# Two more 8 KB slots in a hybrid attention and expert layer: 27 in place of 25, from a smaller descriptor reserve and shared small tiles

## The chip, the cores and the metric

The kernel runs on one core of a Trainium2 chip. The metric is device time in microseconds, the median of several executions; lower is better.

## The reference, cut to what matters

One layer over 256 tokens of width 1024, in float32. Everything but the last step feeds the expert mixture, which reads 96 MB of weights (16 experts of three 2 MB matrices):

```python
xn = rms_norm(h, norm_mix_g)
sb_q, sb_k, sb_v, r_q, r_k, r_v, r_g = split(xn @ w_in)          # 1024 x 4608
y_sb  = stick_breaking_attention(sb_q, sb_k, sb_v) @ w_sb_out
y_ret = silu(r_g) * norm(retention_chunkwise(rotary(r_q), rotary(r_k), r_v)) @ w_ret_out
g_sb, g_ret = split(sigmoid(xn @ w_gate + b_gate))
h = h + (g_sb * y_sb + g_ret * y_ret) @ w_out
hn = rms_norm(h, norm_ffn_g)
# group: top 1 of 4; expert: top 2 of the 4 in the group; combine[t, e] is 0 for the others
for e in range(16):
    hidden = silu(hn @ w_exp_gate[e]) * (hn @ w_exp_up[e])       # 1024 x 512 each
    y = y + combine[:, e:e + 1] * (hidden @ w_exp_down[e])       # 512 x 1024
return rms_norm(h + y, norm_final_g)
```

## The kernel before, in words

SBUF is one pool of equal **slots** of 2048 float32 per partition (8 KB; 1 MB over 128 partitions), handed out by `take` (L120) and returned by `give` (L127). The list of free slots is a queue: the slot that was given back first is taken first. A load of weights, an intermediate result, a work space each take a slot. Small tiles (tables, counts, the router's intermediates) come from a second pool by `small` (L131); two small tiles with the same tag share a place.

Weights are read in tiles of one slot each. `plan` (L154) lists all loads in the order of use; `pump` (L157) issues the next ones, from SyncE's queue, as long as a slot is free and the number of loads so far is below a limit. The table `LIMIT` sets that limit by the number of dense units done (`set_limit`, L734), so that slots are left over for intermediates; from the output projection on (L769) there is no limit, and the free list alone decides. A load that was given the slot of a tile still being read waits on SyncE's queue for the last reader of that tile, and all later loads wait behind it. `drop` (L172) gives a weight tile back after its last use.

The **dense stage** (the first 240 us) splits each weight tile into two float32r halves (ACT copies, DVE subtracts: `split_parts`, L246) and multiplies with both (`mm_unit`, L270), the attention and retention steps between. Then the router ranks each token among its expert's tokens (`choose`, L844; `shares`, L1053). The **expert stage** (`head`, L1094, `tail`, L1145) goes over eight pairs of experts. For pair i the kernel computes the gate product (`proj`, L987: four tiles r = 0 to 3), the up product (four tiles) and, one pair later, the down product (four tiles, `down`, L1019); 64 tokens of each of the two experts form a block of 128 rows. This document calls the tiles of up of pair 0 "up tile 0 to 3 of pair 0", and so on. The order in which the tiles are loaded is gate 0, up 0, then gate i+1, down i, up i+1.

`places` (L951) builds the table that says which token stands in which of the 64 rows; `tables` (L958) transposes it on PE and copies the transpose, 256 columns, to a tile `S` (L972). `scatter` (L1043) multiplies by `S` to add the pair's outputs, `y2`, to the tokens' accumulators. There are two tiles S, used in turns. `after` (L974) runs when PE's products with a tile have been written down: it drops the tile, takes two slots out of those that come free in up of pair 0, one for work space and one for the products `y2`, and calls `pump`:

```python
if not work and key == ("u", 0, 0):
    w = take([P, 2048])
    work.update(b=..., ht=..., pb=..., S=[small([P, T], F32R, "S")])
if not y2 and key == ("u", 0, 3):
    w = take([P, 2048], F32R)
    y2.append(w[:, 0:1024].rearrange("p (h n) -> p h n", h=2))
    work["S"].append(w[:, 1024:1024 + T])
pump()
```

So S of even pairs is a small tile (1 KB, its place shared with `cmp` of `choose`), and S of odd pairs lies in the products' slot.

Of the kernel before, what the change touches and what calls it, by code (L numbers as in the profile page):

```python
# [9 lines left out]
F32 = mybir.dt.float32  # L10
F32R = mybir.dt.float32r
BF16 = mybir.dt.bfloat16
# [5 lines left out]
P = 128  # L18
T = 256
D = 1024  # L20
KC = D // P
NB = T // P
# [1 line left out]
CAP = 64  # L24
PLACE = 1024
EPS = 1e-6
SLOTS = 25

LIMIT = [
    (0, 17), (1, 20), (7, 21), (17, 22), (19, 23), (21, 24), (25, 25), (27, 26), (29, 27), (30, 30),  # L30
    (39, 31), (43, 32), (45, 38), (47, 39), (49, 40), (51, 41), (52, 44), (53, 45), (55, 46), (56, 47),
    (59, 48), (61, 49), (63, 50),
]


# [63 lines left out]
def layer(ctx: ExitStack, tc, cst, dec, prm, x, w_in, w_gate, w_sb_out, w_ret_out,  # L99
          w_out, w_exp_gate, w_exp_up, w_exp_down, out):  # L100
    nc = tc.nc
    pe, act, dve, pool, sp = nc.tensor, nc.scalar, nc.vector, nc.gpsimd, nc.sync
# [12 lines left out]

    free = list(range(SLOTS))
    held = {}
    uid = [0]

    def take(shape=(P, 2048), dt=F32):  # L120
        s = free.pop(0)
        uid[0] += 1
        t = big.tile(list(shape), dt, name=f"b{uid[0]}", tag=f"s{s}")
        held[id(t)] = (s, t)
        return t
# [5 lines left out]
    def small(shape, dt=F32, name=None, bufs=1, tag=None):  # L131
        uid[0] += 1
        return sm.tile(list(shape), dt, name=f"{name}_{uid[0]}", tag=tag or name, bufs=bufs)
# [23 lines left out]
    def pump():  # L157
        while loads and loaded[0] < limit[0] and free:
            key, shape, parts, hook = loads.pop(0)
            t = raws[key] = take(shape)  # L160
            loaded[0] += 1
            for i, (at, src) in enumerate(parts):
                sp.dma_start(t[at], src)
                if hook:
                    hook(i)
# [6 lines left out]
    def drop(key):  # L172
        give(raws.pop(key))
# [315 lines left out]
    key, shape, parts, hook = loads[2]  # L489
# [253 lines left out]
    i = 0  # L743
# [73 lines left out]
    L = small([P, NB, 20], F32, "L")  # L817
    L5 = L.rearrange("p b (g e) -> p b g e", g=5)
    E5 = [P, 5, 4, 4]
    cmp = small([P, NB, 80], F32, "cmp", tag="S")  # L820
    n5 = small([P, NB, 5, 4], F32, "n5")
    gl, en = L[:, :, 0:4], n5[:, :, 1:5, :]
    mask = small([P, NB, 4, 4], BF16, "mask")
# [20 lines left out]
    def choose(tb):  # L844
        stt(L[:, tb, :], lp[:, tb, 0:20], rh[:, tb:tb + 1], par[:, R_BR:R_BR + 20], op0=ALU.mult, op1=ALU.add)
        yield
        c = cmp[:, tb, :]
        c5 = c.rearrange("p (g i j) -> p g i j", g=5, i=4)
        tt(c5, L5[:, tb][:, :, None, :].to_broadcast(E5), L5[:, tb][:, :, :, None].to_broadcast(E5), op=ALU.subtract)
        yield  # L850
        c = c.rearrange("p (a b) -> p a b", b=16)
        tt(c, c, lt[:, None, :].to_broadcast([P, 5, 16]), op=ALU.is_ge)
        dve.tensor_reduce(n5[:, tb].rearrange("p g i -> p (g i)"), cmp[:, tb, :].rearrange("p (a j) -> p a j", j=4),
                          axis=AX.X, op=ALU.add)
        stt(mask[:, tb], en[:, tb], 2.0, n5[:, tb, 0, :][:, :, None].to_broadcast([P, 4, 4]), op0=ALU.is_lt,
            op1=ALU.is_gt)
        m2 = mk[:, tb].rearrange("p (i j) -> p i j", j=2)
        tt(either[:, tb], m2[:, :, 0], m2[:, :, 1], op=ALU.max)
        yield
# [25 lines left out]
    def rows_onto(q, tb):  # L885
        for h in range(2):
            pe.matmul(F[q][tb], identr, hn[h][:, tb, 512 * q:512 * q + 512], start=h == 0, stop=False,
                      skip_group_check=True)

    best, norm = choose(0), row_norm(1)  # L890
    next(best)
    next(norm)
# [10 lines left out]
    rows_onto(1, 0)  # L903
    act.activation(rank[:, 0, :], rp[0][:, 0:8], AF.Copy)
    list(choose(1))
    pe.matmul(rp[1][:, 0:8], tri, either[:, 1, :], start=False, stop=True)
    pe.matmul(rp[1][:, 8:16], ones, either[:, 0, :], start=True, stop=False)
# [13 lines left out]
    def selb(tb):  # L921
        return sel[:, tb, :, None].to_broadcast([P, 4, 4])
# [10 lines left out]
    y2, work, gs = [], {}, {}  # L933
# [40 lines left out]
    def after(key):  # L974
        drop(key)
        if not work and key == ("u", 0, 0):
            w = take([P, 2048])
            work.update(b=w[:, 0:512], ht=[w[:, 512 + 512 * k:1024 + 512 * k].rearrange("p (f s) -> p f s", f=4)
                                           for k in range(2)],
                        pb=w[:, 1536:1664].bitcast(BF16), S=[small([P, T], F32R, "S")])  # L980
        if not y2 and key == ("u", 0, 3):
            w = take([P, 2048], F32R)
            y2.append(w[:, 0:1024].rearrange("p (h n) -> p h n", h=2))
            work["S"].append(w[:, 1024:1024 + T])
        pump()

    def proj(i, which, ps, hook):  # L987
        o = 64 * (i % 4)
        for r in range(4):
            if hook:  # L990
                hook(r)
            w = raws[(which, i, r)]
            for k in range(2):
                c = 2 * r + k
                for j in range(2):
                    pe.matmul(ps[64 * j:64 * j + 64, :], xgt[:, c, o:o + 64], w[:, j, k, :],  # L996
                              start=c == 0, stop=c == KC - 1)
            after((which, i, r))
# [20 lines left out]
    def down(i, hook=None):  # L1019

        ht = work["ht"][i % 2]
        ys = [(bank(b), cs) for b, cs in zip("gm", pieces(i))]
        for r in range(4):
            if hook:
                hook(r)
            w = raws[("d", i, r)]
            j = r // 2
            for y, cs in ys:
                for k in range(2):
                    f = 2 * (r % 2) + k  # L1030
                    for q in range(2):
                        pe.matmul(y[64 * q:64 * q + 64, cs], ht[:, f, 64 * j:64 * j + 64],  # L1032
                                  w[:, k, 512 * q + cs.start:512 * q + cs.stop],
                                  start=r == 0 and k == 0, stop=r == 3 and k == 1)
            after(("d", i, r))
        for y, cs in ys:
            hilo(y2[0][:, 0, cs], y2[0][:, 1, cs], y[:, cs])
# [13 lines left out]
                                  start=False, stop=last and h == 1 and cs.stop == 512, skip_group_check=True)  # L1051

    def shares():  # L1053
        one = [small([P, NB, 4, 4], F32, f"one{k}") for k in range(2)]
        for k in range(2):
            for tb in range(NB):
                stt(one[k][:, tb], en[:, tb], float(k), selb(tb), op0=ALU.is_equal, op1=ALU.mult)
        v = small([P, 2, NB], F32, "v")
        pr = small([P, NB, 16], F32, "pr")
        of = [o.rearrange("p b g e -> p b (g e)") for o in one]  # L1060
        for k in range(2):
            tt(pr, L[:, :, 4:20], of[k], op=ALU.mult)
            dve.tensor_reduce(v[:, k, :], pr, axis=AX.X, op=ALU.add)
        gm = small([P, NB, 1], F32, "gm")
        dve.tensor_reduce(gm, gl, axis=AX.X, op=ALU.max)
        gd = small([P, NB, 4], F32, "gd")
        tt(gd, gl, gm.to_broadcast([P, NB, 4]), op=ALU.subtract)
        act.activation(gd, gd, AF.Exp)
        e2 = small([P, NB], F32, "e2")
        tt(e2, v[:, 1, :], v[:, 0, :], op=ALU.subtract)  # L1070
        act.activation(e2, e2, AF.Exp)
        yield
        gs = small([P, NB], F32, "gs")
        dve.tensor_reduce(gs, gd, axis=AX.X, op=ALU.add)
        den = small([P, NB], F32, "den")
        stt(den, e2, 1.0, gs, op0=ALU.add, op1=ALU.mult)
        dve.reciprocal(den, den)
        yield
        for tb in range(NB):
            c = cm[:, tb, :, 1:3]  # L1080
            pairs = "p (i j) -> p i j"
            stt(pr[:, tb, :], of[1][:, tb, :], e2[:, tb:tb + 1], of[0][:, tb, :], op0=ALU.mult, op1=ALU.add)
            dve.tensor_scalar(c, pr[:, tb, :].rearrange(pairs, j=2), den[:, tb:tb + 1], None, op0=ALU.mult)
            dve.tensor_copy(cm[:, tb, :, 0:1], rh[:, tb:tb + 1][:, :, None].to_broadcast([P, NE // 2, 1]))
        yield
        for a in range(3):
            part = cmb[:, :, :, a, :].rearrange("p b i c -> p (b i) c")
            rest = cm.rearrange("p b i c -> p (b i) c")
            dve.tensor_copy(part, rest)
            if a < 2:  # L1090
                tt(rest, rest, part, op=ALU.subtract)
        yield

    def head(first):  # L1094

        pt = pt0 if first else [onehot(0, tb, rank[:, tb, :]) for tb in range(NB)]
        parts = shares() if first else iter(())
        gather(0, pt, [0])

# [141 lines left out]
```

## Time and profile before

| | |
|---|---|
| median of 3 executions | 463.96 us (463.85 to 464.1) |
| the profiled execution, its own time | 464.75 us |
| its span, first to last instruction | 463.0 us |
| PE (matmul) busy | 443.4 us, 96% |
| PEld (weight loads) busy | 298.8 us, 65% |
| DVE, ACT, POOL busy | 186.9, 166.7, 22.2 us |
| bytes moved | 142.49 MB, mean 308 GB/s |

The profile is one execution. Engines are PE (matmul), PEld (its weight loads), DVE, ACT, POOL and SP (SyncE, whose queue issues the loads). A line such as L996 is a line of the kernel. The page's slices divide the span in 40 equal parts of 11.6 us. Matmuls are pipelined, their ends are modelled, and a float32 product stands as two records: a run of products is read by its first start and last end.

### The profile page before, as it was taken

Reading aid. Unit: us, or ns where it says so; the run is one execution under the profiler, and the core shown is the slowest. Engines: PE = TensorE matmul, PEld = TensorE weight load, DVE = VectorE, ACT = ScalarE, POOL = GpSimd, SP = SyncE. Lnnn points to the kernel's source line nnn. Section 1 sums busy time; section 2 is a strip of 40 time slices with the busy share of each in tenths; the row PEclk is TensorE's granted clock in tenths of the full one; section 3 lists DMA queues with packets and bytes.
Section 4 is the critical chain, followed back from the end, with each engine's and each line's share of the span. In section 5 each row is a group of like instructions: output and inputs, shape, how many; then the busy total and the mean of one; then the engine's idle time right before and its main releaser. Section 6 shows DMA issues by size and latency. Waiting matters only on the chain.

```text
span 463.0 us, 6743 instructions
## 1 busy us (share of the span) xinstructions
PE 443.4 (96%) x2715; PEld 298.8 (65%) x2715; DVE 186.9 (40%) x349; ACT 166.7 (36%) x246; POOL 22.2 (5%) x36
## 2 busy tenths in 40 slices
PE   7999999999999999999999999999989999999881
PEld 6699878888899999999996333333353333333240
DVE  4756487654457865578538410101031001010003
ACT  3643688895653655444543020101000010102003
POOL 2400110110002200000001000000000000000000
PEclk9999999999999999999999999999999999999997
DMA  8999975249302279995949999999999999999972
GB/s 282 353 382 392 388 250 172 90 121 316 107 1 92 92 237 372 408 398 183 368 159 335 346 370 390 410 408 411 408 409 410 409 410 409 409 408 409 410 288 97
DMA packets 58037, 142.49 MB, mean 308 GB/s; under 512 B 3344, under 2 KB 23952, under 8 KB 57872
## 3 DMA queue, kind: packets, MB, share of 16 engines
q1 hardware_dynamic: 57568, 141.35, 81.2%
q10 hardware_dynamic: 432, 0.65, 0.5%
q8 instruction: 23, 0.38, 0.3%
q14 instruction: 14, 0.11, 0.1%
HBM read 140.93 MB, written 1.05 MB: 307 GB/s over the span
## 4 chain that ended last, share of the span: by engine, by line
PE 80%; DMA 14%; DVE 2%; ACT 1%; issue 1%; POOL 1%; SPq 0%; ACTq 0%; DVEq 0%
PE p L294 20%; PE p L996 17%; PE p L1032 8%; PE p L281 8%; PE p L284 7%; PE p L282 7%; DMA b<-in_w_exp_down 6%; DMA b<-in_w_exp_up 5%; DMA b<-in_w_exp_gate 2%; PE p L945 2%; PE z L586 1%; PE p L1050 1%; DMA b<-in_x 1%; PE p L688 1%; PE p L629 1%
## 5 line engine op out<-in xcount | busy, mean ns | idle before, releaser
L253 DVE TENSOR_TENSOR b<-b,b 128x1024 fp32r<-128x1024 f32 x72 | 88.7, 1241 | 71.7 <-ACT b L251 70.6
L996 PE MATMUL p<-b,b 128*64 128x512 f32 x512 | 117.1, 597 | 0.2 <-DMA b<-in_w_exp_up 0.2
L294 PE MATMUL p<-b,b 128*128 128x512 f32 (+1 forms) x504 | 102.7, 359 | 0.5 <-ACT b L251 0.3
L251 ACT ACTIVATE b<-b 128x1024 fp32r<-128x1024 f32 x72 | 75.5, 1056 | 76.6 <-PE p L282 47.7
L294 PEld LDWEIGHTS p<-b,b 128*128 128x128 f32 x504 | 82.6, 190 | 14.6 <-ACT b L251 0.7
L996 PEld LDWEIGHTS p<-b,b 128*64 128x64 f32 x512 | 35.8, 137 | 68.1 <-issue 64.4
L281 PE MATMUL p<-b,b 128*128 128x256 f32 x288 | 71.6, 286 | 0.0
L282 PE MATMUL p<-b,b 128*128 128x256 f32 x288 | 70.7, 283 | 0.0
L1032 PE MATMUL p<-b,b 128*64 128x512 f32 (+1 forms) x288 | 57.8, 548 | 2.7 <-DMA b<-in_w_exp_down 1.9
L281 PEld LDWEIGHTS p<-b,b 128*128 128x128 f32 x288 | 55.1, 191 | 0.5
L282 PEld LDWEIGHTS p<-b,b 128*128 128x128 f32 x288 | 55.2, 192 | 0.0
L1032 PEld LDWEIGHTS p<-b,b 128*64 128x64 f32 x288 | 20.2, 137 | 38.5 <-issue 32.3
L284 PE MATMUL p<-b,b 128*128 128x256 f32 x288 | 41.1, 283 | 0.0
L573 DVE SCALAR_TENSOR_TENSOR b<-p,b 128x512 fp32r<-128x512 f32 (+1 forms) x13 | 7.4, 566 | 83.3 <-ACT b L572 83.3
L284 PEld LDWEIGHTS p<-b,b 128*128 128x128 f32 x288 | 37.4, 192 | 0.0
L1011 DVE SCALAR_TENSOR_TENSOR b<-p,share,b 128x512 f32<-128x512 f32 x8 | 6.0, 751 | 62.6 <-PE p L996 62.6
L572 ACT ACTIVATE b<-p 128x512 fp32r<-128x512 f32 (+1 forms) x13 | 6.4, 495 | 53.5 <-PE p L1032 52.9
L972 ACT ACTIVATE b<-p 128x256 fp32r<-128x256 bf16 x4 | 1.5, 386 | 38.1 <-PE p L971 38.1
L972 ACT ACTIVATE S<-p 128x256 fp32r<-128x256 bf16 x4 | 1.5, 384 | 37.4 <-PE p L971 37.4
L1006 ACT ACTIVATE b<-p,share 128x512 f32<-128x512 f32 x8 | 5.5, 688 | 21.3 <-PE p L996 21.3
L1017 ACT ACTIVATE b<-p 128x512 f32<-128x512 f32 x8 | 4.8, 597 | 22.9 <-PE p L1016 22.9
L1188 POOL TENSOR_TENSOR rf<-rf,mhalf 128x1 f32<-128x1 f32 x2 | 1.1, 542 | 208.1 <-DVE rf L1187 208.1
(172 smaller groups left out, 338.2 us busy)
## 6 DMA issues: line engine op xcount, KB each, us to landing
b<-in_w_exp_gate SPq DMA_DIRECT2D x64, 512.0 KB, 10.2
b<-in_w_exp_up SPq DMA_DIRECT2D x64, 512.0 KB, 10.2
b<-in_w_exp_down SPq DMA_DIRECT2D x31, 1024.0 KB, 12.7
b<-in_w_in SPq DMA_DIRECT2D x17, 1024.0 KB, 14.3
b<-in_w_gate SPq DMA_DIRECT2D x8, 1024.0 KB, 5.3
b<-in_w_ret_out SPq DMA_DIRECT2D x4, 1024.0 KB, 5.0
b<-in_w_out SPq DMA_DIRECT2D x4, 1024.0 KB, 11.5
b<-in_w_sb_out SPq DMA_DIRECT2D x2, 1024.0 KB, 9.4
```

Source lines behind the costliest of these rows:

```text
L251: act.activation(hi, raw, AF.Copy)
L253: tt(lo, raw, hi.bitcast(F32), op=ALU.subtract)
L281: pe.matmul(ps, wh[:, k, cs], h[:, k, :], start=k == 0, stop=False)
L282: pe.matmul(ps, wh[:, k, cs], l[:, k, :], start=False, stop=False)
L284: pe.matmul(ps, wl[:, k, cs], h[:, k, :], start=False, stop=k == nk - 1)
L294: pe.matmul(ps[tb], kth(a, k)[:, tb * P:(tb + 1) * P], b[:, j, :], start=n == 0 and k == 0, stop=n == 2 and k == KC - 1)
L572: act.activation(hi, src, AF.Copy)
L573: stt(lo, src, 1.0, hi.bitcast(F32), op0=ALU.mult, op1=ALU.subtract)
L945: pe.matmul(ps[:, c, :], hn[h][:, tb, features(c2, c)], pt[tb].rearrange("p e s -> p (e s)"), start=c == 0 and tb == 0 and h == 0, stop=c ...
L996: pe.matmul(ps[64 * j:64 * j + 64, :], xgt[:, c, o:o + 64], w[:, j, k, :], start=c == 0, stop=c == KC - 1)
L1011: stt(work["b"], u, gs[i][:, 0:1], work["b"], op0=ALU.mult, op1=ALU.mult)
L1032: pe.matmul(y[64 * q:64 * q + 64, cs], ht[:, f, 64 * j:64 * j + 64], w[:, k, 512 * q + cs.start:512 * q + cs.stop], start=r == 0 and k == ...
```

## The change

It makes 27 slots of 8 KB in place of 25. The room comes from two sides. The program is built with a reserve of 1 KB per partition for the descriptors of transfers that GpSimd would issue, in place of the default 16 KB. And small tiles are put together: both tiles S lie in the products' slot, which is now taken when up tile 1 of pair 0 is dropped, and no longer tile 3; `cmp` is one tile of 96 numbers for both blocks of tokens, in which the tiles `one` and `pr` of `shares` lie too. All limits rise by 2.

```diff
-SLOTS = 25
+SLOTS = 27
 LIMIT = [
-    (0, 17), (1, 20), (7, 21), (17, 22), (19, 23), (21, 24), (25, 25), (27, 26), (29, 27), (30, 30),
+    (0, 19), (1, 22), (7, 23), (17, 24), (19, 25), (21, 26), (25, 27), (27, 28), (29, 29), (30, 32),
...
-    cmp = small([P, NB, 80], F32, "cmp", tag="S")
+    cmp = small([P, 96], F32, "cmp")
...
-        c = cmp[:, tb, :]
+        c = cmp[:, 0:80]
...
-                        pb=w[:, 1536:1664].bitcast(BF16), S=[small([P, T], F32R, "S")])
-        if not y2 and key == ("u", 0, 3):
+                        pb=w[:, 1536:1664].bitcast(BF16))
+        if not y2 and key == ("u", 0, 1):
             w = take([P, 2048], F32R)
             y2.append(w[:, 0:1024].rearrange("p (h n) -> p h n", h=2))
-            work["S"].append(w[:, 1024:1024 + T])
+            work["S"] = [w[:, 1024 + T * k:1024 + T * k + T] for k in range(2)]
...
-        one = [small([P, NB, 4, 4], F32, f"one{k}") for k in range(2)]
+        one = [cmp[:, 32 * k:32 * k + 32].rearrange("p (b g e) -> p b g e", b=NB, g=4) for k in range(2)]
...
-        pr = small([P, NB, 16], F32, "pr")
+        pr = cmp[:, 64:96].rearrange("p (b e) -> p b e", b=NB)
...
-    nc = _bacc.Bacc("TRN2", target_bir_lowering=False, num_devices=1)
+    nc = _bacc.Bacc("TRN2", target_bir_lowering=False, num_devices=1, dynamic_dma_scratch_size=1024)
```

The order of instructions on each engine stays; what moves is the moment at which a load is written into the program, and with it the slot that it gets. On SyncE's queue, the loads of down of pair 1 (four) and of up of pair 2 (four, each in two halves) stood like this before. The first number in a tile's name counts tiles in the order in which the kernel's code makes them: a tile that is made earlier is one for which a slot came free earlier.

```order
L163 DMA b270_2569<-in_w_exp_down 128x2x1024
L163 DMA b271_2580<-in_w_exp_down 128x2x1024
L163 DMA b275_2597<-in_w_exp_down 128x2x1024
L163 DMA b279_2615<-in_w_exp_down 128x2x1024
L163 DMA b282_2630<-in_w_exp_up 128x1024 x2
L163 DMA b283_2637<-in_w_exp_up 128x1024 x2
L163 DMA b288_2661<-in_w_exp_up 128x1024 x2
L163 DMA b289_2668<-in_w_exp_up 128x1024 x2
```

And with the change:

```order
L163 DMA b263_2527<-in_w_exp_down 128x2x1024
L163 DMA b267_2548<-in_w_exp_down 128x2x1024
L163 DMA b269_2570<-in_w_exp_down 128x2x1024
L163 DMA b270_2581<-in_w_exp_down 128x2x1024
L163 DMA b277_2614<-in_w_exp_up 128x1024 x2
L163 DMA b278_2621<-in_w_exp_up 128x1024 x2
L163 DMA b280_2632<-in_w_exp_up 128x1024 x2
L163 DMA b281_2639<-in_w_exp_up 128x1024 x2
```

Before, the four down loads took the slots of gate tiles 2 and 3 and up tiles 1 and 2 of pair 0, and the work space and the products took those of up tiles 0 and 3 (names 273 and 280). With the change the four down loads take the slots of gate tiles 0 to 3 of pair 0, the work space and the products those of up tiles 0 and 1 (272 and 273), and the first load of up of pair 2 that of up tile 2; from the third on, each load has the slot that a load two places ahead of it had before.

On ACT the copies of the transposed place tables (L972) stood like this, with what each waits for in brackets (DMAHW: a transfer's landing); `b_2589` is the work space and `b_2621` the products' slot:

```order
L972 ACTIVATE S_2590<-p_2606 128x256 [waits PE_49]
L1006 ACT_TABLE_LOAD [waits DMAHW5_49,DMAHW4_49]
L1006 ACTIVATE b_2589<-p_2489,share_2602 128x512 [waits DVE_49]
L972 ACTIVATE b_2621<-p_2647 128x256 [waits DMAHW3_49,DMAHW2_49,PE_49]
L1017 ACTIVATE b_2589<-p_2651 128x512 [waits PE_49]
```

And with the change, where `b_2597` is the products' slot:

```order
L972 ACTIVATE b_2597<-p_2605 128x256 [waits DMAHW7_49,DMAHW6_49,PE_49]
L1006 ACT_TABLE_LOAD [waits DMAHW5_49,DMAHW4_49]
L1006 ACTIVATE b_2590<-p_2495,share_2601 128x512 [waits DVE_49]
L972 ACTIVATE b_2597<-p_2649 128x256 [waits PE_49]
L1017 ACTIVATE b_2590<-p_2653 128x512 [waits PE_49]
```

The first copy now goes to a slot that held a weight tile, so it waits for that tile's two transfers, which the second copy did before; no other wait is added.

## Rows read from the trace of the kernel before

**Rows 1.** The page's slices: PE's busy tenths, and GB/s moved.

```profile
PE   7999999999999999999999999999989999999881
...
GB/s 282 353 382 392 388 250 172 90 121 316 107 1 92 92 237 372 408 398 183 368 159 335 346 370 390 410 408 411 408 409 410 409 410 409 409 408 409 410 288 97
```

**Rows 2.** Waits of PE, 20 to 245 us: total, times, longest.

```profile
PE p L553 <- POOL rxp L317: 0.5, 1, 0.5
```

**Rows 3.** PE's timeline, 418 to 453 us: start, us, instruction, records, [idle before].

```profile
418.03 6.71 PE L996 MATMUL p<-b,b 128*64 128x512 f32 x26
424.96 1.93 PE L996 MATMUL p<-b,b 128*64 128x512 f32 x6 [0.22 <-DMA b<-in_w_exp_up]
...
427.84 4.17 PE L996 MATMUL p<-b,b 128*64 128x512 f32 x16
432.74 1.94 PE L1032 MATMUL p<-b,b 128*64 128x512 f32 x8 [0.72 <-DMA b<-in_w_exp_down]
...
437.07 0.66 PE L1016 MATMUL p<-identr,b 128*128 128x128 f32 x4
...
440.32 1.94 PE L1032 MATMUL p<-b,b 128*64 128x512 f32 x8 [0.63 <-DMA b<-in_w_exp_down]
442.98 1.95 PE L1032 MATMUL p<-b,b 128*64 128x256 f32 x16 [0.71 <-ACT b L572]
...
445.98 5.94 PE L1032 MATMUL p<-b,b 128*64 128x256 f32 x48
```

**Rows 4.** The chain that ended last, its end: start, us, what.

```profile
421.14 11.46 DMA b<-in_w_exp_down
...
434.68 15.69 DMA b<-in_w_exp_down
...
450.41 1.52 PE p L1032 x12
```

**Rows 5.** Stretches: length, busy time by engine, PE clock, DMA share, GB/s.

```profile
266.00:268.00 2.00, 2.00 (x12) 0.61 (x10) 0.25 (x2) 1.97 (x3) 0.00 (x0) 1.00 0.95 266
268.00:280.00 12.00, 11.87 (x62) 4.15 (x60) 1.62 (x6) 1.92 (x4) 0.00 (x0) 1.00 1.02 391
...
300.00:385.00 85.00, 83.25 (x418) 31.21 (x416) 11.08 (x28) 8.09 (x14) 0.00 (x0) 1.00 1.03 409
```

**Rows 6.** Waits of SyncE's queue over the span: total, times, longest.

```profile
SPq L163 <- PE p L996: 26.0, 19, 3.2
```

**Rows 7.** SyncE's timeline, single issues: start, us of issue, what.

```profile
259.64 0.38 SPq L163 DMA_DIRECT2D b<-in_w_exp_down  x1
261.36 0.38 SPq L163 DMA_DIRECT2D b<-in_w_exp_down  x1
265.60 0.37 SPq L163 DMA_DIRECT2D b<-in_w_exp_down  x1
267.74 0.37 SPq L163 DMA_DIRECT2D b<-in_w_exp_down  x1
271.17 0.34 SPq L163 DMA_DIRECT2D b<-in_w_exp_up  x1
272.89 0.33 SPq L163 DMA_DIRECT2D b<-in_w_exp_up  x1
275.81 0.33 SPq L163 DMA_DIRECT2D b<-in_w_exp_up  x1
```

**Rows 8.** PE's timeline, 249 to 300 us, two runs of 32 records.

```profile
265.76 7.09 PE L996 MATMUL p<-b,b 128*64 128x512 f32 x32
...
277.32 7.04 PE L1032 MATMUL p<-b,b 128*64 128x512 f32 x32
```

**Rows 9.** DMA issues, 235.3 to 235.5 us: one half tile, median us to landing.

```profile
b<-in_w_exp_up SPq DMA_DIRECT2D x1, 512.0 KB, 3.2
```

**Rows 10.** Line L972: what ended ACT's idle time before its copies (us, times).

```profile
  PE p L971: 75.5, 8
```

**Rows 11.** The page's DMA queues: packets, MB, share of 16 engines.

```profile
q1 hardware_dynamic: 57568, 141.35, 81.2%
```

More of the change, by code (lines that the diff above doesn't have):

```diff
@@ L26 @@
 EPS = 1e-6
-SLOTS = 25
+SLOTS = 27
 LIMIT = [
-    (0, 17), (1, 20), (7, 21), (17, 22), (19, 23), (21, 24), (25, 25), (27, 26), (29, 27), (30, 30),
-    (39, 31), (43, 32), (45, 38), (47, 39), (49, 40), (51, 41), (52, 44), (53, 45), (55, 46), (56, 47),
-    (59, 48), (61, 49), (63, 50),
+    (0, 19), (1, 22), (7, 23), (17, 24), (19, 25), (21, 26), (25, 27), (27, 28), (29, 29), (30, 32),
+    (39, 33), (43, 34), (45, 40), (47, 41), (49, 42), (51, 43), (52, 46), (53, 47), (55, 48), (56, 49),
+    (59, 50), (61, 51), (63, 52),
 ]
@@ L852, in choose @@
         tt(c, c, lt[:, None, :].to_broadcast([P, 5, 16]), op=ALU.is_ge)
-        dve.tensor_reduce(n5[:, tb].rearrange("p g i -> p (g i)"), cmp[:, tb, :].rearrange("p (a j) -> p a j", j=4),
+        dve.tensor_reduce(n5[:, tb].rearrange("p g i -> p (g i)"), cmp[:, 0:80].rearrange("p (a j) -> p a j", j=4),
                           axis=AX.X, op=ALU.add)
```

## The prediction

> **What bounds the kernel now.** I read the page's slices first. TensorE is at 7 to 9 tenths in every slice [rows 1], so busy shares alone name no bound; the GB/s line says more. Counted from 0, it falls to 1 and 92 in slices 11 to 13, is still 159 in slice 20, and from slice 25 to slice 37 it stands at 408 to 411 [rows 1]. So the transfers have long idle stretches early on and are saturated at the end.
>
> Second, who waits. From 20 to 245 us PE waited for another engine once, for 0.5 us [rows 2]: the dense stages are bound by PE, and loads that come earlier there buy nothing by themselves. In the last expert pairs it is different. A run of 32 expert records, four tiles, takes 7.09 or 7.04 us when nothing is missing [rows 8]. At 418.03 us the next 32 (26 and 6) are done at 424.96 + 1.93 = 426.89 instead of 425.12, 1.77 late; the 16 from 427.84 take 4.17 against half of 7.09, 0.62 late; the down product of pair 6 runs from 432.74 to 440.32 + 1.94 = 442.26, where it needs 7.04 and 0.66 for four transposes, 1.8 late, and starts 0.73 after the 432.01 at which the 16 ended [rows 3]. That is 4.9 us of waiting, named as waits for expert weights in the same rows; the 0.71 before 442.98 is ACT's and stays. The final run of 48 half records takes 5.94 against 3 x 1.95, so it holds next to nothing more than the last load's own wait [rows 3].
>
> Third, the chain. Its last link before PE is a load that was issued at 434.68 and took 15.69 us, to 450.37; PE follows with 1.52, and 12.6 us of products, norm and stores end the span at 463.0 [rows 4]. A load that takes 15.69 us is not a slow load: it stands in a full queue. So the question is not when this load is issued but when the stream of loads last stood still, because from there to the end it runs at its own rate: 266 GB/s from 266 to 268 us, 391 from 268 to 280, then 409 for 85 us [rows 5]. One tile of 1 MB (128 x 8 KB = 1.049 MB) is 2.56 us at 409 GB/s, and PE needs 1.72 for it (272.89 - 271.17) [rows 7]. DMA is the slower of the two, and PE eats the store of tiles loaded ahead until about 421 us.
>
> Fourth, what held the stream back before 268. SyncE waited 26.0 us in 19 waits for expert products [rows 6], that is for a slot to come free. The issues show it: 271.17, 272.89 and so on [rows 7] are PE's tile ends, 265.76 + 7.09 = 272.85 being one of them [rows 8].
>
> **The change, part by part.** *Two more slots.* Tile n of the stream waits for the slot of tile n - 25 now and of n - 27 then, since the limits rise by the same 2 up to the expert stage and bind nothing after it. Number the tiles from the fourth down tile of pair 1, place 0. A release at time t for place k forces the end of the stream to at least t - 2.56 k plus a constant; the largest such number rules. Before [rows 7]: place -3, 259.64 + 7.68 = 267.32; -2, 261.36 + 5.12 = 266.48; -1, 265.60 + 2.56 = 268.16; 0, 267.74; 1, 271.17 - 2.56 = **268.61**; 2, 272.89 - 5.12 = 267.77; 3, 275.81 - 7.68 = 268.13. Later places fall, since PE frees slots each 1.72 us and the stream takes 2.56.
>
> If every release moved to a place two later, each number would fall by 5.12. It does not quite come so, because of the second edit.
>
> *Both place tables in the products' slot.* The products' slot is taken when the second up tile of pair 0 is dropped, no longer the fourth. Before, the releases of tiles 0 and 3 went to work space and those of 1 and 2 to the loads of places -1 and 0. Now 0 and 1 go to work space, and 2 and 3 to places 1 and 2. So the numbers are: 259.64 at place -1, 262.20; 261.36 at 0; 267.74 at 1, **265.18**; 269.45 (one tile of 1.71 after 267.74) at 2, 264.33; 271.17 at 3, 263.49; 272.89 at 4, 262.65; 275.81 at 5, 263.01. The ruling number falls from 268.61 to 265.18, by **3.43 us**. In words: up tile 0 of pair 2 is issued at 267.74 and not at 271.17, and from it on the stream never stops.
>
> [...]
>
> The bounds of this term: below, if the issue at 271.17 was in truth covered by the loads still queued and 268.16 ruled, 2.98. Above, the stream also lost bytes from 268 to 280: 391 against 409 is (1 - 391/409) x 12 = 0.5 us, which a deeper queue may win back, so 3.9 to 4.3. I take 3.43, as the releases give it.
>
> *Does PE pass it on?* It must still be waiting for loads after the shift: 4.9 us of waits are there, 3.43 is less. So the end moves with the last load, from 450.37 to 446.9, and the 12.6 us behind it stay. Past some 4.9 to 5 us PE would be the bound; that caps any gain.
>
> *The table copies* on ACT now write into the products' slot, eight times. In all eight ACT waited for the transpose on PE, in none for the products in the same slot, though four of the copies were in it already [rows 10]. The two waits for transfers that the first copy gets are for weights that PE has multiplied with by then. Zero; if a copy did wait for a scatter, the scatter before it on PE is over by then in program order.
>
> *cmp, one and pr in one small tile*: the same DVE instructions in the same order, with waits for DVE alone as before. The work is in front of the first expert product, so a delay there would move every release by as much: the largest price I see is one small DVE step, about 0.25 us off the gain. I take zero.
>
> *The loads before the expert stage* run two further ahead, behind a PE that does not wait [rows 2]; the first loads keep their places in the queue. Zero, and SyncE's row of issues has the same length. *The reserve*: the transfers are of the hardware queue of SyncE [rows 11]. Zero.
>
> The sum is -3.43 us. The profiled execution took 464.75 (span 463.0), which is 0.79 over the median of 463.96; against itself it would be 461.3, against the median **460.5**. The likeliest case's own range is 3.0 to 4.3 less: 459.7 to 461.0.
>
> **The rivals.** *The whole two slots, 5.12 us: 458.8.* It needs the wait for 267.74 hidden by 265.18 - 263.49 = 1.7 us of queued loads, two thirds of a tile. For it: a lone half tile lands 3.2 us after its issue, where its bytes need 1.28 [rows 9], so some waits overlap with bytes under way. Against it: PE's 4.9 us would be used up at about the same point, and the two tiles issued at 259.64 and 261.36 have 5.1 us of bytes, and with the 1.9 us (3.2 - 1.28) between an issue and its bytes they are done by 266.7; the bytes of the issue at 267.74 start about 269.6. Chance 0.15.
>
> *Nothing: 464.* The extra slots would go to tiles other than loads, or PE would be the bound at the end already. Against it: the order of the changed program shows the same loads made earlier, and PE waits by name for weights in the last 30 us [rows 3]. Chance 0.07.
>
> *Slower, through the transfers' rate.* The reserve is cut to a sixteenth and every slot lies elsewhere; if the loads used that reserve, fewer would be in flight. From 269 to 448 us the stream runs at its rate for 179 us, so a rate lower by 1.9%, 401 for 409 GB/s, costs 3.4 us and eats the gain; that is the deciding point. With two half tiles in flight, 1.049 MB in each 3.2 us [rows 9], it would be 328 GB/s: 179 x (409/328 - 1) = 44 us, 504 in all. Against it: nearly all bytes are on the hardware queue [rows 11], and POOL issues no transfer. [...] Chance 0.04.
>
> **How the numbers follow.** Forecast 0.74, full two slots 0.15, nothing 0.07, slower 0.04. The time is that of the forecast, 460.5. The range runs from the full gain, 458.8, to 461.3, a little above the lower bound of the term (461.0) for the 0.25 us of DVE. Faster by over 0.2% (0.9 us, about what a measurement can tell from no change): 0.89; within: 0.07; slower: 0.04.
>
> **What would show it.** Right: up tile 0 of pair 2 is issued at about 267.7, the fourth down tile of pair 1 at 261.4, the GB/s line has a dip to well under 409 at about 267 to 269.5 that is deeper than now, and none after it; the last load lands near 447; PE's waits for weights after 421 fall to some 1.5 us. Wrong: a rate of the last 170 us away from 409; the last load earlier by 3.4 but the span not; a copy of a table that waits for a scatter; or the dip absent, and the whole 5.1 there.

## The result and the profile after

The changed kernel takes 460.33 us (median of 4, 459.6 to 460.77) against 464.01 for the kernel before in the same comparison: a ratio of 0.992, 95% interval 0.9907 to 0.9935, that is 3.7 us less (3.0 to 4.3). The profiled execution took 460.21 us, its span is 458.5. Four later comparisons put the median of the kernel before at 464.4 to 465.0; its first three runs, against which the forecast was made, lie low among these.

The page's slices of the changed kernel, PE's busy tenths and GB/s, against [rows 1]:

```profile
PE   7899999999999999999999999999989999999991
...
GB/s 280 353 381 387 393 356 272 91 95 315 140 1 93 39 240 394 408 390 186 362 188 291 338 306 411 408 410 410 408 409 410 408 409 408 410 407 410 410 302 98
```

The dip is in slice 23 (306, where 370 stood), after which the stream is at its 409 as before; PE's slices 37 and 38 are 9 and 9, where they were 8 and 8. SyncE's timeline of the changed kernel, start, us of issue, what (x2: both half tiles), against [rows 7]:

```profile
261.30 0.37 SPq L163 DMA_DIRECT2D b<-in_w_exp_down  x1
267.68 0.82 SPq L163 DMA_DIRECT2D b<-in_w_exp_up  x2
269.40 0.80 SPq L163 DMA_DIRECT2D b<-in_w_exp_up  x2
```

The fourth down tile of pair 1 is issued at 261.30, not 267.74, and up tile 0 of pair 2 at 267.68, not 271.17. Between them the queue stands on one release, the longest wait in SyncE's row, 5.9 where [rows 6] had 3.2 (total us, times, longest):

```profile
SPq L163 <- PE p L996: 27.3, 18, 5.9
```

The sum of that row has grown, from 26.0 to 27.3, while the kernel became faster: what counts is which of the waits is the last that starves the queue. The stretches of the changed kernel, last column GB/s, against [rows 5]:

```profile
266.00:268.00 2.00, 2.00 (x12) 0.67 (x10) 0.19 (x2) 1.97 (x3) 0.00 (x0) 1.00 0.40 164
268.00:280.00 12.00, 11.87 (x62) 4.13 (x60) 1.62 (x6) 1.86 (x4) 0.00 (x0) 1.00 0.95 358
...
300.00:385.00 85.00, 83.26 (x418) 31.18 (x416) 11.07 (x28) 8.08 (x14) 0.00 (x0) 1.00 1.03 409
```

Fewer bytes move from 266 to 280 than before, since more of them had moved earlier; from 300 on the rate is the same. PE's timeline of the changed kernel at the end (start, us, instruction, records, [idle before]), against [rows 3]. In both kernels the loads end in the order gate 7, up 7, down 6, down 7, not in that of the pairs before (down 3, too, comes ahead of gate 4), and the last tile comes in two halves:

```profile
417.98 7.09 PE L996 MATMUL p<-b,b 128*64 128x512 f32 x32
...
426.01 3.65 PE L996 MATMUL p<-b,b 128*64 128x512 f32 x16
429.50 3.60 PE L1032 MATMUL p<-b,b 128*64 128x512 f32 x16
433.03 0.66 PE L1016 MATMUL p<-identr,b 128*128 128x128 f32 x4
433.62 3.91 PE L1032 MATMUL p<-b,b 128*64 128x512 f32 x16
438.24 1.95 PE L1032 MATMUL p<-b,b 128*64 128x256 f32 x16 [0.71 <-ACT b L572]
...
441.26 5.99 PE L1032 MATMUL p<-b,b 128*64 128x256 f32 x48
```

The 32 records that took 1.77 too long before now take their 7.09, and the 16 that took 4.17 take 3.65: PE has run into the end of its store of tiles only at about 434, not 421. The chain's end, against [rows 4]:

```profile
430.02 15.67 DMA b<-in_w_exp_down
445.73 1.51 PE p L1032 x12
```

The last load lands at 445.69, 4.68 earlier than before, and the end follows it.

### The profile page after: what moved, and what is told of

It is laid out like the page before. It is cut to its first block, busy times and chain, and to the rows that moved or that the text cites. A ratio compares the mean times of both kernels' runs of the same rounds, so it can differ in the third digit from the quotient of the medians.

```text
span 458.5 us, 6741 instructions
## 1 busy us (share of the span) xinstructions
PE 440.3 (96%) x2715; PEld 297.7 (65%) x2715; DVE 186.7 (41%) x349; ACT 166.7 (36%) x246; POOL 22.1 (5%) x36
## 4 chain that ended last, share of the span: by engine, by line
PE 90%; DMA 4%; DVE 2%; ACT 1%; issue 1%; POOL 1%; SPq 0%; ACTq 0%; DVEq 0%
PE p L996 25%; PE p L294 20%; PE p L1032 9%; PE p L281 8%; PE p L284 8%; PE p L282 8%; DMA b<-in_w_exp_down 3%; PE p L945 2%; PE p L1050 2%; PE z L586 1%; DMA b<-in_x 1%; PE p L1016 1%; PE p L688 1%; PE p L629 1%; PE z L617 1%
## 5 line engine op out<-in xcount | busy, mean ns | idle before, releaser
L996 PE MATMUL p<-b,b 128*64 128x512 f32 x512 | 115.1, 596 | 0.0
L996 PEld LDWEIGHTS p<-b,b 128*64 128x64 f32 x512 | 35.1, 137 | 66.6 <-issue 63.8
L1032 PE MATMUL p<-b,b 128*64 128x512 f32 (+1 forms) x288 | 57.5, 547 | 0.9 <-ACT b L572 0.7
L1032 PEld LDWEIGHTS p<-b,b 128*64 128x64 f32 x288 | 20.2, 137 | 36.0 <-issue 31.5
L972 ACT ACTIVATE b<-p 128x256 fp32r<-128x256 bf16 x8 | 3.1, 383 | 75.5 <-PE p L971 75.5
L945 PEld LDWEIGHTS p<-pt,b 128*128 128x128 f32 x64 | 8.1, 195 | 4.4 <-DVE pt L863 2.3
```

Source lines behind the costliest of these rows:

```text
L945: pe.matmul(ps[:, c, :], hn[h][:, tb, features(c2, c)], pt[tb].rearrange("p e s -> p (e s)"), start=c == 0 and tb == 0 and h == 0, stop=c ...
```

## The experiments

All times are medians in us, with the lowest, the highest and the number of runs; "before" is the kernel before in the same comparison, the interval is that of the ratio.

| run | time | before | ratio, 95% |
|---|---|---|---|
| the change again | 460.22 (459.39 to 460.92, 4) | 464.98 | 0.9886 to 0.9914 |
| exchange alone, 25 slots | 465.86 (465.46 to 466.93, 11) | 464.98 | 1.0014 to 1.0037 |
| 26 slots | 463.12 (463.03 to 464.66, 6) | 464.98 | 0.9951 to 0.9978 |
| products' slot late, reserve 128 | 458.77 (457.8 to 458.88, 4) | 464.98 | 0.9843 to 0.9873 |
| small reserve, 25 slots | 464.34 (463.48 to 465.05, 12) | 464.44 | 0.9988 to 1.001 |
| old limits, 27 slots | 460.17 (459.29 to 460.84, 5) | 464.44 | 0.9885 to 0.9917 |
| the change, reserve 128 | 458.93 (457.29 to 459.08, 4) | 464.44 | 0.9849 to 0.9892 |
| before, reserve 15488 | 460.88 (459.5 to 461.6, 6) | 464.44 | 0.9903 to 0.9937 |
| before, reserve 15872 | 464.3 (463.73 to 465.69, 10) | 464.58 | 0.998 to 1.0006 |
| before, reserve 15424 | 464.97 (464.21 to 465.63, 10) | 464.58 | 0.9992 to 1.0019 |
| before, reserve 15616 | 464.38 (463.74 to 465.28, 10) | 464.39 | 0.9987 to 1.001 |
| products' slot later still, reserve 128 | 458.18 (457.37 to 458.94, 4) | 464.58 | 0.9833 to 0.9882 |

The theory is the prediction's: the end of the stream follows max(release - 2.56 x place). The first four runs were meant to split it into its two terms.

**The change again.** No edit.

> The changed kernel once more, as the measure for the others of this call. Both theories: 460.3, 3.7 us under the kernel before.

460.22, up tile 0 of pair 2 issued at 267.48: repeated.

**The exchange alone.** The changed kernel with the 25 slots and the limits of before:

```diff
-SLOTS = 27
+SLOTS = 25
```

> 25 slots and the limits of before, with all the other edits (both tables in the products' slot, taken at up tile 1 of pair 0). Theory of places: the release of up tile 2 goes to place -1, 267.74 + 2.56 = 270.30, that of up tile 3 to place 0; against 268.61 before, the stream ends 1.69 us later: 465.7. Rival (the exchange costs nothing): 464.0.

SyncE's timeline of this kernel:

```profile
267.52 0.37 SPq L163 DMA_DIRECT2D b<-in_w_exp_down  x1
269.23 0.37 SPq L163 DMA_DIRECT2D b<-in_w_exp_down  x1
270.95 0.34 SPq L163 DMA_DIRECT2D b<-in_w_exp_up  x1
```

The release that should serve place 0 now serves place -1, as worked out: the third down tile goes out at 267.52, the fourth at 269.23. The kernel is slower by 0.14 to 0.37%, 0.7 to 1.7 us. The edit that gives up the small tile for a place in the products' slot has a price, and the theory's 1.69 is at the upper end of it.

**26 slots.** The same edit with `SLOTS = 26` and limits one higher than before.

> 26 slots and limits one above those of before, with all the other edits. Theory of places: up tile 2's release at place 0 rules with 267.74, only 0.87 under the 268.61 of before: 463.1. Rival (each slot is worth 1.7 to 1.8 us): 462.2.

SyncE's timeline of this kernel:

```profile
267.62 0.37 SPq L163 DMA_DIRECT2D b<-in_w_exp_down  x1
269.34 0.82 SPq L163 DMA_DIRECT2D b<-in_w_exp_up  x2
```

Each slot moves the same release one place on. From 25 to 26 to 27 slots with the exchange the medians go 465.86, 463.12, 460.22, steps of 2.7 and 2.9 where one tile is 2.56: a slot was worth about one tile of stream here, as long as the stream was the bound.

The steps are the theory's, the distance to the kernel before is not quite. By the ratios the three lie 1.2 us above (0.7 to 1.7), 1.7 below (1.0 to 2.3) and 4.6 below it (4.0 to 5.3), where the theory has 1.69 above, 0.87 and 3.43 below: each 0.5 to 1.2 lower. So it is luck that 463.12 met 463.1, which was worked out from 464.0, and for 26 slots the time alone would suit the rival, with 1.7 to 1.8 a slot. The rival fails in the other two of this comparison: by it the exchange costs nothing and 27 slots bring 3.4. The issue times are the theory's in all three.

**The products' slot late.** 27 slots, that slot taken after the fourth up tile as before and one S a small tile again; its room comes from a reserve of 128 bytes:

```diff
-        if not y2 and key == ("u", 0, 1):
+        if not y2 and key == ("u", 0, 3):
...
-dynamic_dma_scratch_size=1024)
+dynamic_dma_scratch_size=128)
```

> 27 slots, but the products' slot is taken at up tile 3 of pair 0 again, and the even table is a small tile again (the reserve is cut to 128 bytes to make room). Theory of places: up tiles 1 and 2 of pair 0 go to loads at places 1 and 2, the gate tile 0 of pair 1 to place 3; the ruling number is 263.49 in place of 265.18, so the stream ends 1.69 us earlier than with the change: 458.7 if PE passes it on, up to 459.2 if PE becomes the bound at about 5 us under the kernel before. First up load of pair 2 at about 265.6. Rival, each slot is worth PE's 1.72 us for a tile and the exchange costs nothing: 460.3, as with the change.

458.77 is what was forecast, and up tile 0 of pair 2 went out at 265.40 (forecast 265.6), but the trace says that the time came about in another way. The stretch from 300 to 385 us, last column GB/s, and then PE's timeline of this kernel, with ACT's copy of the products of pair 6:

```profile
300.00:385.00 85.00, 83.25 (x416) 31.10 (x414) 11.08 (x28) 8.09 (x14) 0.00 (x0) 1.00 1.03 419
```

```profile
425.88 3.65 PE L996 MATMUL p<-b,b 128*64 128x512 f32 x16
429.37 3.60 PE L1032 MATMUL p<-b,b 128*64 128x512 f32 x16
432.90 0.66 PE L1016 MATMUL p<-identr,b 128*128 128x128 f32 x4
...
435.68 3.18 PE L1032 MATMUL p<-b,b 128*64 128x512 f32 x22
437.25 0.60 ACT L572 ACTIVATE b<-p 128x512 fp32r<-128x512 f32 x1 [2.98 <-PE p L1032]
```

The loads ran at 419 GB/s, which neither theory had, and PE waits for no weights any more (from 285 to 457 us it waited 1.5 us in all, for DVE): it is the bound. So this run does not measure the exchange's price apart from the rate. It raised a question of its own, which the next runs take up, and it shows what PE's line looks like without a missing tile.

**Small reserve, 25 slots.** The kernel before with two of the change's edits that move no load, the reserve of 1 KB and the shared small tile:

> The kernel with 25 slots and the old limits, the products' slot taken after the fourth up tile and the first place table in a tile of its own as before; only the reserve is 1 KB and the three small tables of the routing share one tile. Places theory: neither edit moves a load, so 464.0 us like the kernel before (within 0.7), the down tile 3 of pair 1 issued near 268.6, loads at 409 GB/s. Rival 'the loads use the reserve': a rate below 401 GB/s in the expert stage and over 465 us.

464.34 against 464.44; the rate is 409, and up tile 0 of pair 2 goes out at 271.03 as in [rows 7]. The fourth down tile goes out at 267.60, also as before; the 268.6 of the expectation is the ruling number, not an issue time. The reserve's size as such does nothing to these loads: 409 GB/s with 1 KB as with 16 KB.

**Old limits.** The changed kernel with the `LIMIT` table of before.

> The changed kernel with the table of limits of the kernel before. Places theory: the limits bind in the dense stage, where TensorE is the bound, and the first load that takes one of the two further places is the up tile 0 of pair 2, long after the last limit; so 460.3 us (459.6 to 460.9), with that tile issued at 267.5 to 267.7. Rival 'the limits carry a part of the gain' (expert loads of pair 0 and 1 start earlier by two tiles): the tile is issued later than 268.5 and the time is above 461.2.

460.17, with that tile issued at 267.47: the limits carry nothing.

**The change with a reserve of 128 bytes.** `dynamic_dma_scratch_size=128`, nothing else.

> The changed kernel with a reserve of 128 bytes, nothing else: every slot begins at 128 bytes past a multiple of 8 KB, not at 1 KB past it. In the run with the later products' slot, which had 128 bytes too, the loads ran at 419 GB/s and not at 409. Theory R (the reserve's size or the slots' place does it): 419 GB/s here as well from 300 to 385 us, the last weights landing near 441.5 instead of 445 to 445.7, and 458.5 to 459.2 us with TensorE as the bound of the end. Rival (the later products' slot or the first place table's own tile does it): 409 GB/s, last landing near 445, 460.3 us.

From 300 to 385 us this kernel ran at 419 as well, and the chain's end (start, us, what) holds no load:

```profile
300.00:385.00 85.00, 83.25 (x418) 31.18 (x416) 11.08 (x28) 8.08 (x14) 0.00 (x0) 1.00 1.03 419
```

```profile
433.87 5.31 PE p L1032 x32
440.31 5.33 PE p L1032 x48
```

PE waits 1.5 us from 285 to 457 us, for DVE again and not for weights. The products' slot is not what raised the rate.

**The kernel before, with a reserve of 15488 bytes.** In the programs as built the reserve comes first in SBUF, at byte 0, and every tile lies behind it, so this moves every tile, and nothing else. 15488 is nearly the old size:

```diff
-num_devices=1)
+num_devices=1, dynamic_dma_scratch_size=15488)
```

> The kernel before with a reserve of 15488 bytes, not 16384, nothing else: the slots begin 128 bytes past a multiple of 1 KB as in the run with 128 bytes, and the reserve is nearly whole. Theory 'the slots' place in memory sets the rate': 419 GB/s, 70 tiles that each take 0.06 us less, last landing near 446, 460.0 us or below. Rival 'the size of the reserve sets it' (or neither): 409 GB/s, 464.0 us.

460.88: a kernel with 25 slots and all waits of before gains as much as the whole change does, by where its tiles lie. The rate (419) and the last landing (446.34) came as the first theory had them; the time is 0.9 over its 460.0. The queue's row from 300 to 385 us (packets, MB, share of 16 engines' time), first of the kernel before, then of this one:

```profile
q1 hardware_dynamic: 9371, 34.69, 102.3%
```

```profile
q1 hardware_dynamic: 9605, 35.56, 102.3%
```

The DMA engines are busy the same share of the time and move 2.5% more packets in it: each packet takes less (an estimated 145 ns on average, not 148: 16 engines x 85 us x 1.023, over the packets), the queue is no fuller. Its tile issues lie where those of before do (up tile 0 of pair 2 at 271.07).

The expectations of this run, of the one before it and of the next three take the slots to begin where the reserve ends. They do not: in the programs as built 128 bytes of constants lie between the two. So the slots of this kernel begin at 15616, which is 61 x 256, those of the kernel before at 16512, 128 past a multiple of 256.

**Other starts.** Reserves of 15872, 15424 and 15616 bytes.

> The kernel before with a reserve of 15872 bytes: the slots begin 512 bytes past a multiple of 1 KB. In the run with a shift of 128 bytes the loads ran at 419 GB/s. Theory 'a slot must not begin at a multiple of 1 KB': 419 GB/s here too and 460.9 us. Rival 'it must not begin at a multiple of 512 bytes or less': 409 GB/s, 464.2 us.

> The kernel before with a reserve of 15424 bytes: the slots begin 64 bytes past a multiple of 1 KB. Theory 'any place off the multiple of 1 KB does': 419 GB/s and 460.9 us. [...]

> The kernel before with a reserve of 15616 bytes: the slots begin 256 bytes past a multiple of 1 KB. Shifts of 0, 64 and 512 bytes left the loads at 409 GB/s, one of 128 gave 419. Theory 'an odd multiple of 128 bytes is wanted': 409 GB/s and 464.2 us. Rival 'any multiple of 128 bytes that is none of 512': 419 GB/s and 460.9 us.

The stretch from 300 to 385 us of these three kernels, in that order:

```profile
300.00:385.00 85.00, 83.25 (x418) 31.10 (x414) 11.09 (x28) 8.08 (x14) 0.00 (x0) 1.00 1.03 409
```

```profile
300.00:385.00 85.00, 83.25 (x418) 31.14 (x416) 11.08 (x28) 8.08 (x14) 0.00 (x0) 1.00 1.03 409
```

```profile
300.00:385.00 85.00, 83.25 (x418) 31.10 (x414) 11.08 (x28) 8.08 (x14) 0.00 (x0) 1.00 1.03 409
```

All three 409, and no gain in time. With the constants counted, this is where the slots begin in each kernel:

| reserve | slots begin at | past a multiple of 256 | GB/s, 300 to 385 us |
|---|---|---|---|
| 16384 (before) | 16512 | 128 | 409 |
| 1024 (the change, and 25 or 26 slots) | 1152 | 128 | 409 |
| 15872 | 16000 | 128 | 409 |
| 15424 | 15552 | 192 | 409 |
| 15616 | 15744 | 128 | 409 |
| 15488 | 15616 | 0 | 419 |
| 128 (all three kernels with it) | 256 | 0 | 419 |

The two starts at a multiple of 256 bytes give 419, the five others 409. The readings that the expectations tried (a multiple of 1 KB, any shift, an odd multiple of 128) all counted from starts that are 128 too low, and none of them holds. Both fast starts are odd multiples of 256; no start at a multiple of 512 was tried.

**The products' slot later still.** The run with 128 bytes and the late slot, taken now after the second gate tile of pair 1:

```diff
-        if not y2 and key == ("u", 0, 3):
+        if not y2 and key == ("g", 1, 1):
```

> The run with the later products' slot and 128 bytes, with that slot taken later still, after the second gate tile of the second expert: up tile 0 of pair 2 is issued near 263, not 265.4, and the last landing comes 2 us earlier than 440.75. TensorE waited for no weight in that run's expert stage, so theory 'TensorE is the bound now': 458.7 us, within 0.3 of that run. Rival 'places still pay': 457 us or less.

Up tile 0 of pair 2 went out at 264.80, not near 263, and my figure was wrong: in both runs that tile has the slot of up tile 1 of pair 0, and all loads of this run up to there go out 0.6 earlier. What the edit moves are up tiles 2 and 3 of pair 2, from 270.96 to 268.65 and from 272.68 to 270.37. The last load landed at 440.44, only 0.31 earlier than with the late slot, and the time, 458.18, has an interval that covers that run's. PE is the bound (0.0 us of waiting before the expert products, L996 and L1032), and places pay no more. It, the late slot and the plain change with a reserve of 128 bytes are all faster than both kernels; they cannot be told apart by these runs.

## Why the prediction was right, and where its sizes were off

**The bound and the mechanism were right.** The stream of loads ends the kernel, its rate is unchanged at 409, and what matters is the last release that starves it. The issue times came to 0.1 us: 261.30 (forecast 261.4) and 267.68 (267.7). The dip at 266 to 268 is 164 GB/s where [rows 5] had 266. The runs with 25, 26 and 27 slots show the release at 267.5 to 267.7 passing from the third down tile to the fourth to the up tile.

**The term of 3.43 was somewhat small.** In the profiled executions the last landing moved by 4.68. The landing of up tile 3 of pair 2 had moved by 3.65 of these; the rest arose later, in the steady stream. Of that stretch, from there to the last landing, the five profiles at 409 GB/s with 25 slots and the release times of before took 164.1 to 165.1 us (mean 164.6), the three with 27 slots 163.9 to 164.1. So some 0.7 us of the gain arose behind the releases that the sum counts; with so few profiles, whose ranges touch, this is not certain, but it is about what the runs with 25 to 27 slots lie below the theory. The 0.5 that the prediction's upper bound would win back from 268 to 280 did not come there: 358 GB/s, not 391. In the time, the ratio of the first comparison gives 3.7 (3.0 to 4.3), that of the change run again 4.0 to 5.3. The forecast of 460.5 met 460.33 in part because it was set against three runs of before that lie low. Where the 0.7 comes from was not tried. In the profile of before two landings in that stretch are late by 0.6 and 1.1 us, each behind a packet of the instruction queue that held one DMA engine for about 1 us. That is not shown to be the cause: the changed kernel has such packets at the same times (304.0 and 330.5 us) with no late landing behind them.

**The cap on PE's side was mis-sized.** The prediction put PE's waits at 4.9 us and said that "the 0.71 before 442.98 is ACT's and stays". The trace of the change names ACT again for 0.71 before 438.24. But the first down tile of pair 7, issued at 421.53, took 16.6 us (DMA issues of the changed kernel, that issue alone):

```profile
b<-in_w_exp_down SPq DMA_DIRECT2D x1, 1024.0 KB, 16.6
```

It landed at 438.1, 0.14 before PE began, and before it was 426.26 + 16.6 = 442.86, again just ahead of the 442.98. In the run with the products' slot late, where that tile was there in time, PE ran on through the copy (22 records from 435.68 to 438.86, the copy from 437.25 to 437.85). And in the kernel before with the reserve of 15488, where the tile landed at 438.56, PE began before the copy's end at 438.72:

```profile
438.12 0.60 ACT L572 ACTIVATE b<-p 128x512 fp32r<-128x512 f32 x1 [3.73 <-PE p L1032]
438.70 1.95 PE L1032 MATMUL p<-b,b 128*64 128x256 f32 x16 [0.69 <-DMA b<-in_w_exp_down]
```

So the wait was for weights and the name was that of the event that came last by a hair. In the run with the products' slot late the final run of 48 half records takes 5.40, not 5.94, so it held 0.5 of waiting too. From the start of the 32 records at about 418 to the end of the last down product it takes 445.33 - 417.85 = 27.5 us in that run; in the kernel before it was 451.92 - 418.03 = 33.9 and after the change 447.25 - 417.98 = 29.3. So PE waited 6.4 us in all, not 4.9 (the 0.71 and the 0.5 are most of what was missed), and 1.8 are left (the forecast said some 1.5). The difference, 4.6, is about what the change brought in the profiled executions, 464.75 - 460.21 = 4.5.

**The edits costed at nothing cost nothing.** Reserve and shared tile together: 464.34 against 464.44. Limits: 460.17 against 460.22 to 460.33. The copies of S into the products' slot waited for PE alone, as in [rows 10] (line L972 of the changed kernel, now one group of eight):

```profile
L972 ACT ACTIVATE b<-p 128x256 fp32r<-128x256 bf16 x8 | 3.1, 383 | 75.5 <-PE p L971 75.5
```

**The rivals.** The full 5.12 fell: the wait for the release at 267.7 was not hidden, as the 164 GB/s from 266 to 268 show; the time alone, 4.0 to 5.3 in the change run again, would not exclude it. The slower one fell with the reserve's run: with 1 KB the rate was 409 GB/s and the time 464.34 against 464.44. Yet its remark that "every slot lies elsewhere" touched something real, in the other direction: where the slots lie changed the rate by 2.5% up, not in this change, whose slots still begin 128 past a multiple of 256, but with a reserve of 128 or 15488 bytes.

**The rate.** It is 409 or 419 GB/s from 300 to 385 us in every run.

## What to carry to other kernels

When a stream of loads runs at its full rate to the end, give each tile a place, subtract place times the tile's time from the release that it waits for, and look at the largest: a slot was worth about one tile's transfer here (2.56 us by the rate, steps of 2.7 and 2.9 in time), and the edit that hands a slot to work space earlier cost some of it again (0.7 to 1.7). Before the places are reshuffled, look up in the built program where the tiles begin: the start at 15616, a multiple of 256 bytes, brought as much as the whole change (3.6 us and 3.7), and the change with a start at 256 brought 5.5, not 7.3, since TensorE became the bound. A wait's named releaser is to be checked against the landing time of the load beside it.

## What the runs showed of the hardware that I had not expected

In these runs the rate of the loads, in packets of 4 KB (8468 of 9371 in the kernel before, the rest under 512 bytes), went with where the destination tiles begin in SBUF: 419 GB/s from 300 to 385 us where the slots begin at a multiple of 256 bytes (256 and 15616), 409 where they begin 128 past one (1152, 15744, 16000, 16512) or 192 past one (15552). With 25 slots the share of busy time is the same, 102.3% at a start of 16512 and of 15616, for 9371 and 9605 packets, so single packets are quicker, by about 2.5%. The rate at 192 past is that at 128 past. Why a start off the multiple is slower, no run shows.
